# A two-layer diffusion transformer: the first loads cut into quarters of the columns, each with its products, in a written order

## The chip, the cores and the metric

The kernel runs on one core of a Trainium2 chip. The time is device microseconds (us) of that core, lower is better. Five engines work side by side: TensorE (PE: products, transposes), VectorE (DVE), ScalarE (ACT), GpSimd (POOL) and SyncE (SP), each with its own queue that it works off in order; PEld is TensorE's weight load. SP and ACT also start DMA transfers.

## What is computed

Two layers of a hybrid block act on 512 tokens of `x` and 256 context tokens of `ctx`, 1024 columns wide. Each has a SwiGLU feed-forward of half weight, a mixer of four parts (S5 scans, neighbourhood attention, grouped attention, RG-LRU), and another feed-forward. Shifts, scales and gates come from the conditioning vectors. Only the start of the first feed-forward matters here:

```python
def ffn_half(h, g, w_i, w_o, shift, scale, gate):
    y = modulate(rms_norm(h, g), shift, scale)      # rms_norm(h, g) * (1 + scale) + shift
    a, b = jnp.split(y @ w_i, 2, axis=-1)
    return h + FFN_RES * gate * ((jax.nn.silu(a) * b) @ w_o)

ml = ada_mods(silu(c), w_ada[l], b_ada[l], dt)      # mods 0 and 1: shift and scale of 1024 columns each
```

Everything is float32.

## The kernel before

The residual lies in SBUF transposed: eight tiles `e` of 128 columns by 768 tokens (512 latent, 256 context). A float32 product is made of three products of the operands' two parts: high (`wh`, `g` as cast) and low (`wl`, `g` as the difference): hi by lo', lo by hi', hi by hi'. `wload` brings a weight tile, `wsplit` splits it: the cast to `wh` on ACT (L378), the difference `wl` on DVE (L379). There are two buffers each of `wh` and `wl`. `mm` (L389) makes the products.

The feed-forward runs over 22 column tiles `f`. Each has two halves, a and b, in two PSUM tiles `pi` out of two; a half is 8 row blocks x 3 products x 2 pieces. One piece is 258 columns wide (2 for the shifts, of the latent and the context tokens, and tokens 0 to 255), the other 512 (tokens 256 to 767). The RMS factor isn't applied to the input but to the products: `z = pi * R` (L449, L453), where `R` is the factor spread over the partitions. So a `pi` comes free only when `R` is there. `bc` (L448) takes the shifts' products out of `pi`.

At the start the modulations of the first layer are made on TensorE, in two steps of `ada_first`, the scales first and the shifts later. Loads `l`, `z` of 128 x 512 (L206), products with two columns `s` into `pa` (L215), copies to `z` on ACT (L223), transposes to `pt` (L226), sums with the bias to `mods` on DVE (L238). The rows come as 128 tokens x 512 columns (`load_rows`, L168) and are transposed for each of the eight tiles (L178), copied (L180) and squared (`sq_tile`); the squares are summed on DVE. Then `hg_tile` makes the modulated residual's parts: `g` high on ACT (L304), low on DVE (L305). With `in_pair` the first column tile makes its 512-column products of both halves, then calls `setup_rest`, which makes the shifts (`hg_shift`, L291 and L292, the two columns of `g` ahead of the tokens) and the RMS factor (`rms_factor`: `pr` sums over the partitions L357, the inverse root by small steps on DVE L344 to L350, `pb` and its copy to `R` L364 to L366), and then its 258-column products.

The order on each engine is set by a scheduler that moves instructions between the lines as written, by dependencies and its own costs; `tc.keep_in_program_order` (new in the change) keeps an instruction where the program writes it. DMAs on SP and ACT go out in the order of their queue. The S5 coefficients (`S5Coef`, from L1350 on) are made of many small steps on DVE that the scheduler puts where there is room; they are needed much later.

Of the kernel before, what the change touches and what calls it, by code (L numbers as in the profile page):

```python
# [15 lines left out]
P = 128  # L16
D = 1024
NT = D // P
# [16 lines left out]
class Net:  # L35
    def __init__(self, ctx, tc, A, out):
# [11 lines left out]
        self.uid = 0  # L48

# [11 lines left out]
    def setup(self):  # L61
# [22 lines left out]
        scale = self.ada_first(2, 2, "llllllllllllzzzz")  # L84
        raws = [[], []]
        for i, f in enumerate(scale):
            f(0)
            for j in range(6 * i, 6 * i + 6):
                if j < 12:
                    raws[j // 6].append(self.load_rows(j % 6, j // 6))  # L90
        self.load_vectors(0, self.FIRST)
        for f in scale:
            f(1)
        self.transpose_rows(raws)
        gs = self.gain_scale(0, "g_ffn1", 1)
# [18 lines left out]
    def load_rpb(self):  # L114
        """the neighbourhood's biases with something to read before and after them"""
# [13 lines left out]
    def load_vectors(self, l, names=None):  # L129
        """rows to columns; of a layer's rows the first ones or those after them"""  # L130
# [24 lines left out]
        if l == 2:  # L155
            self.s2 = self.const.tile([P, NT, 2], F32, name="s2")
            for i in range(2):
                nc.scalar.activation(self.s2[:, :, i], self.cols[2][:, 8 * i:8 * i + 8], AF.Silu)

# [4 lines left out]
    def load_rows(self, t, b):  # L164
        """128 tokens' half"""
        raw = self.t("g")
        src = self.A["x"][0, t * P:(t + 1) * P, :] if t < 4 else self.A["ctx"][0, (t - 4) * P:(t - 3) * P, :]
        self.nc.sync.dma_start(raw[:, :512], src[:, b * 512:(b + 1) * 512])  # L168
        return raw

    def transpose_rows(self, raws):
        nc = self.nc
        self.h = []
        for j in range(NT):
            ps = self.psb.tile([P, 1024], F32, name=self.nm("px"), tag="psb")
            for t in range(6):
                o = (j % 4) * P
                nc.tensor.transpose(ps[:, t * P:(t + 1) * P], raws[j // 4][t][:, o:o + P], self.ident)  # L178
# [1488 lines left out]
```

## Time and profile before

| | |
|---|---|
| median of 3 runs | 2879.89 us (2878.98 to 2880.39) |
| span of the profiled execution | 2877.7 us |
| TensorE busy | 2819.1 us, 98% of the span |
| VectorE busy | 1742.3 us, 61% |
| ACT busy | 906.5 us, 32% |
| GpSimd busy | 757.7 us, 26% |

The profile is of one execution. Its times are microseconds from the start of the span. TensorE's clock is shown as granted, 1.00 is 2.4 GHz and 0.50 is 1.2 GHz. A plain float32 product on TensorE (`pa`, `pt`, `pr`, `pb`) stands in the trace as two passes, a product of two parts (`pi`) as one.

### The profile page before, as it was taken

The numbers are of one execution on the slowest core, as the hardware profiler recorded it, in microseconds if no ns is written. First come the engines' busy times: TensorE is split into PE (matmuls) and PEld (weight loads), VectorE is DVE, ScalarE is ACT, GpSimd is POOL, SyncE is SP. The second block draws the span as 40 slices with busy tenths as digits, with TensorE's granted clock in tenths as the row PEclk, the third lists the DMA queues.
The fourth block names the chain that finished last, engine by engine and source line by source line (L and its number), as shares of the span: only waits on it lengthen the run. The fifth ranks groups of instructions, "written<-read, shape, count | busy, mean of one in ns | idle before, by whom it ended". The sixth has DMA issues, their size and how long they took to land.

```text
span 2877.7 us, 43478 instructions
## 1 busy us (share of the span) xinstructions
PE 2819.1 (98%) x17293; PEld 2437.7 (85%) x17293; DVE 1742.3 (61%) x3178; ACT 906.5 (32%) x1478; POOL 757.7 (26%) x957
## 2 busy tenths in 40 slices
PE   7999999999999999999999999999999999999998
PEld 4888888888877888888888888888888887899998
DVE  6868577676857566363634766465466876444445
ACT  4212121235546422112123321222224645322223
POOL 2822233221323311000001176332312434201001
PEclk9999999999999999999999999999999999999999
DMA  6445324353323333222311335233254343232231
GB/s 227 134 108 167 112 96 141 123 185 118 115 62 74 103 115 99 87 96 95 107 54 54 118 101 142 80 123 106 74 168 145 118 106 89 79 96 83 88 96 52
DMA packets 295901, 312.13 MB, mean 108 GB/s; under 512 B 58991, under 2 KB 243202, under 8 KB 295698
## 3 DMA queue, kind: packets, MB, share of 16 engines
q1 hardware_dynamic: 266990, 293.97, 31.8%
q0 software_dynamic: 5664, 12.59, 1.9%
q10 hardware_dynamic: 23044, 2.78, 0.7%
q8 instruction: 137, 2.24, 0.3%
q14 instruction: 66, 0.54, 0.1%
HBM read 276.09 MB, written 29.02 MB: 106 GB/s over the span
## 4 chain that ended last, share of the span: by engine, by line
PE 88%; DVE 6%; DMA 2%; ACT 2%; issue 1%; POOL 0%; SPq 0%; ACTq 0%; DVEq 0%; POOLq 0%
PE pi L389 51%; PE po L389 23%; PE po L1236 4%; DVE acc L256 2%; PE po L862 2%; PE pt L810 2%; DMA wa<-in_w_ada_dram 1%; PE ps L793 1%; PE pa L263 1%; DVE wl L379 1%; PE ps L794 1%; DMA l<-in_w_ada_dram 1%; PE pl L734 1%; DVE z L455 0%; PE pa L215 0%
## 5 line engine op out<-in xcount | busy, mean ns | idle before, releaser
L389 PE MATMUL pi<-g,wh 128*128 128x258 f32 (+2 forms) x6656 | 1408.7, 330 | 8.4 <-ACT wh L378 2.6
L389 PEld LDWEIGHTS pi<-g,wh 128*128 128x128 f32 x6656 | 1101.4, 191 | 132.2 <-issue 15.0
L389 PE MATMUL pi<-g,wl 128*128 128x258 f32 (+2 forms) x3328 | 828.1, 329 | 0.7 <-DVE wl L379 0.7
L378 ACT CAST wh<-wr 128x1024 fp32r<-128x1024 f32 (+3 forms) x380 | 338.2, 890 | 1397.4 <-PE pi L389 674.8
L389 PEld LDWEIGHTS pi<-g,wl 128*128 128x128 f32 x3328 | 607.4, 191 | 60.6 <-issue 2.5
L389 PE MATMUL po<-l,wh 128*128 128x512 f32 (+1 forms) x2464 | 566.1, 344 | 0.9 <-DVE e L495 0.8
L389 PEld LDWEIGHTS po<-l,wh 128*128 128x128 f32 x2464 | 387.9, 188 | 63.9 <-issue 3.9
L459 POOL TENSOR_TENSOR l<-z,l 128x768 fp32r<-128x768 f32 (+1 forms) x88 | 159.1, 1808 | 1061.4 <-ACT l L458 955.4
L379 DVE TENSOR_TENSOR wl<-wr,wh 128x1024 fp32r<-128x1024 f32 (+3 forms) x380 | 407.0, 1071 | 50.3 <-ACT wh L378 47.5
L256 DVE SCALAR_TENSOR_TENSOR acc<-wa,s,acc 128x512 f32<-128x512 f32 x448 | 358.6, 849 | 39.4 <-DMA wa<-in_w_ada_dram 38.6
L495 DVE SCALAR_TENSOR_TENSOR e<-po,gt,e 128x512 f32<-128x512 f32 (+1 forms) x296 | 176.2, 631 | 307.4 <-PE po L389 250.7
L389 PE MATMUL po<-l,wl 128*128 128x512 f32 (+1 forms) x1232 | 337.5, 343 | 1.0 <-DVE wl L379 1.0
L453 DVE TENSOR_TENSOR z<-pi,R 128x768 f32<-128x768 f32 (+2 forms) x91 | 78.4, 865 | 301.3 <-PE pi L389 301.3
L389 PEld LDWEIGHTS po<-l,wl 128*128 128x128 f32 x1232 | 194.5, 188 | 32.6 <-DVE wl L379 2.0
L448 DVE COPY bc<-pi 128x2 f32<-128x2 f32 x88 | 13.7, 156 | 189.4 <-PE pi L389 189.4
L458 ACT CAST l<-z 128x768 fp32r<-128x768 f32 (+1 forms) x88 | 68.8, 782 | 160.5 <-DVE z L455 160.5
L1545 POOL TENSOR_TENSOR ww<-AR,BB 128x256 f32<-128x256 f32 x32 | 25.9, 808 | 341.4 <-PE pw L1564 309.5
L455 DVE SCALAR_TENSOR_TENSOR z<-z,pi,z 128x512 f32<-128x512 f32 (+1 forms) x154 | 107.1, 730 | 5.5 <-ACT z L451 0.7
L317 POOL TENSOR_TENSOR ssq<-ssq,sq 128x768 f32<-128x768 f32 (+1 forms) x35 | 67.5, 1929 | 161.0 <-ACT sq L316 161.0
L451 ACT ACTIVATE z<-z,bc 128x512 f32<-128x512 f32 (+1 forms) x154 | 90.0, 625 | 62.7 <-DVE z L449 51.3
L449 DVE TENSOR_TENSOR z<-pi,R 128x768 f32<-128x768 f32 (+1 forms) x88 | 77.5, 880 | 3.7 <-ACT R L366 3.7
L1236 PE MATMUL po<-l,wh 128*128 128x512 f32 (+1 forms) x264 | 71.9, 356 | 0.0
(349 smaller groups left out, 2632.0 us busy)
## 6 DMA issues: line engine op xcount, KB each, us to landing
wr<-in_w_ffn_in_dram SPq DMA_DIRECT2D x88, 1024.0 KB
wa<-in_w_ada_dram SPq DMA_DIRECT2D x64, 1024.0 KB
wr<-in_w_ffn_out_dram SPq DMA_DIRECT2D x48, 512.0 KB
wr<-in_w_ffn_out_dram SPq DMA_DIRECT2D x32, 640.0 KB
wr<-in_w_in_dram SPq DMA_DIRECT2D x16, 1024.0 KB
W<-s5w SPq DMA_DIRECT2D x32, 256.0 KB
wr<-in_w_out_dram SPq DMA_DIRECT2D x8, 1024.0 KB
l<-in_w_ada_dram SPq DMA_DIRECT2D x24, 256.0 KB
```

The source lines that it names most:

```text
L256: nc.vector.scalar_tensor_tensor(acc[r], raw[:, k], s, acc[r], ALU.mult, ALU.add)
L378: nc.scalar.copy(hi[:, :kn], raw[:, :, o:o + P])
L379: nc.vector.tensor_sub(lo[:, :kn], raw[:, :, o:o + P], hi[:, :kn].bitcast(F32))
L389: nc.tensor.matmul(dst, lhsT=wt[:, k, :], rhs=xt[:, a:b], start=(k == 0 and i == 0), stop=(k == kn - 1 and i == 2))
L449: nc.vector.tensor_mul(ta[:, :nt], pa[:, 256:256 + nt], self.R[:, :nt])
L451: nc.scalar.activation(ta[:, a:b], ta[:, a:b], AF.Silu, bias=bc[:, i:i + 1])
L453: nc.vector.tensor_mul(tb[:, a:b], p, self.R[:, a:b])
L455: nc.vector.scalar_tensor_tensor(tb[:, a:b], tb[:, a:b], pb[:, 254 + i:255 + i], ta[:, a:b], ALU.add, ALU.mult)
L458: nc.scalar.copy(uh[:, :nt], tb[:, :nt])
L459: nc.gpsimd.tensor_sub(ul[:, :nt], tb[:, :nt], uh[:, :nt].bitcast(F32))
L495: self.nc.vector.scalar_tensor_tensor(self.h[j][:, a:b], ps[:, a:b], gate[:, j, i:i + 1], self.h[j][:, a:b], ALU.mult, ALU.add)
L1236: self.nc.tensor.matmul(dst, lhsT=wt[:, k, :], rhs=xt[:, a:b], start=(c == 0 and i == 0), stop=(c == NT - 1 and i == 2))
```

## The change

- **Loads.** `ada_first` now makes 256 columns at a time: loads of 3, 3 and 2 row blocks (128x3x256), `pa` of 32 x 256 in strips of 32 rows, one copy to `z` on ACT, and a small product with `sel`, which adds the strips up and transposes in one. The rows come as 256 columns at a time. SP's order is: quarter 0 of the scales, quarter 0 of the rows, the first two weight tiles (128x8x128, of column tile 0 alone), quarters 1 to 3, then the shifts.
- **Scale quarters.** `setup` makes for each quarter the scale, two tiles `e`, two tiles `g`, and the 512-column products of the quarter ahead, in an order pinned on TensorE, ACT and DVE.
- **Shift quarters.** `setup_rest` makes for each quarter the shifts, two times `hg_shift`, and the 12 products of 258 columns. These products are not pinned.
- **Column tiles 0 and 1** have weights of their own, loaded at 128 columns; from tile 2 on the weights come in pairs, as before.
- **Squares** of the first tiles are made where the program has room, and summed on DVE.
- The first steps of the S5 coefficients are pinned, behind the transposes of their rows.

```diff
-        scale = self.ada_first(2, 2, "llllllllllllzzzz")
...
+        scale = [self.ada_first(1024 + 256 * c) for c in range(4)]
+        raws = []
+        for c in range(4):
+            scale[c][0]()
+            raws.append(self.load_rows(c))
+            if c == 0:
+                w_in = self.A["w_ffn1_in"][0]
+                self.first = [self.wload(w_in, 0, NT, o, P) for o in (0, DFF)]
...
+        quarter(0)
+        w = [self.wsplit(raw, NT, 0) for raw in self.first]
+        self.first = [(self.psb.tile([P, 1024], F32, name=self.nm("pi"), tag="psb"), x) for x in w]
+        for c in range(4):
+            for j in (2 * c, 2 * c + 1):
+                self.hg_tile(j, 0, None, gs, TT)
+            if c < 3:
+                quarter(c + 1)
+            for k in (2 * c, 2 * c + 1):
+                for ps, x in self.first:
+                    self.mm(self.in_chunks(ps, TT)[1:], x, self.hgx, NT, k, k + 1, self.pin)
         for j in range(NT):
-            self.hg_tile(j, 0, None, gs, TT)
+            self.sq_tile(j, TT, nc.vector)
 
     def setup_rest(self):
...
-        for f in self.ada_first(0, 4, "l" * 12 + "z" * 4):
-            f()
-        for j in range(NT):
-            self.hg_shift(j, 0, 0)
+
+        nc = self.nc
+        shift = [self.ada_first(256 * c) for c in range(4)]
+        for load, _ in shift:
+            load()
+        for c, (_, work) in enumerate(shift):
+            work()
+            for j in (2 * c, 2 * c + 1):
+                self.hg_shift(j, 0, 0)
+                for ps, x in self.first:
+                    self.mm(self.in_chunks(ps, TT)[:1], x, self.hgx, NT, j, j + 1)
         self.rms_factor(TT)
...
+        def work():
+            ps, arow = self.bank("pa")[:, :256], self.t("z")[:, :256]
+            for k in range(NT):
+                o = 32 * (k % 4)
+                self.pin(nc.tensor.matmul(ps[o:o + 32], lhsT=self.s2w[:, 2 * k:2 * k + 32], rhs=w[k], start=(k < 4), stop=(k >= 4)))
+            self.pin(nc.scalar.copy(arow, ps))
+            pt = self.bank("pt", "pst")[:, :4]
+            for b in range(2):
+                self.pin(nc.tensor.matmul(pt[:, 2 * b:2 * b + 2], lhsT=arow[:, b * P:(b + 1) * P], rhs=self.sel, start=True, stop=True))
+            self.ada_add(0, c0 // P, [pt.rearrange("p (q b r) -> p q b r", q=1, r=2)], self.pin)
```

ACT's order where the residual's parts begin. Before, all eight tiles' copies and squares, and the scales, stand ahead of this place:

```order
L223 COPY z_184<-pa_167 2x512 x2
L304 ACTIVATE g_290<-e_201,gs_288 128x512
L304 ACTIVATE g_290<-e_201,gs_288 128x256
L378 CAST wh_350<-wr_346 128x1024
L304 ACTIVATE g_296<-e_211,gs_288 128x512
L304 ACTIVATE g_296<-e_211,gs_288 128x256
L304 ACTIVATE g_302<-e_223,gs_288 128x512
L304 ACTIVATE g_302<-e_223,gs_288 128x256
L378 CAST wh_354<-wr_348 128x1024
```

After, the same place on ACT, from the first weight on (`ssq` takes the first tile's squares, `sq` the others'; `lrow` and `dt` are small loads for the S5 coefficients):

```order
L400 CAST wh_203<-wr_127 128x1024
L245 COPY z_166<-pa_165 128x256
L1374 DMA lrow_963<-in_s_lambda_im_dram 32x64
L1376 DMA dt_968<-in_s_log_step_dram 128x32
L400 CAST wh_207<-wr_129 128x1024
L213 COPY e_181<-px_182 128x512
L335 ACTIVATE ssq<-e_181 128x768
L213 COPY e_192<-px_193 128x512
L338 ACTIVATE sq_424<-e_192 128x768
L326 ACTIVATE g_213<-e_181,gs_164 128x512
L326 ACTIVATE g_213<-e_181,gs_164 128x256
```

Both casts of weights now stand ahead of the first copy of `e`, and the copy of the first scales stands behind the first cast.

TensorE's order at the shifts. Before, one block of sums for all shifts, then the roots' sums `pr`, then all 258-column products (the order goes on so to the 34th of them, where `pb` stands):

```order
L215 MATMUL pa_416<-z_449,s_102 2x512
L215 MATMUL pa_416<-z_451,s_102 2x512
L226 MATMUL pt_463<-ident,z_457 128x128 x4
L357 MATMUL pr_486<-ones,ssq 128x1 x6
L389 MATMUL pi_358<-g_291,wh_350 128x258
L389 MATMUL pi_358<-g_290,wl_351 128x258
L389 MATMUL pi_358<-g_290,wh_350 128x258
```

After, between the products of quarter 0 and of quarter 1 of the shifts, on TensorE:

```order
L411 MATMUL pi_212<-g_219,wl_208 128x258
L411 MATMUL pi_212<-g_219,wh_207 128x258
L244 MATMUL pa_508<-l_459,s2w 32x256 x3
L244 MATMUL pa_508<-l_461,s2w 32x256 x3
L244 MATMUL pa_508<-l_463,s2w 32x256 x2
L248 MATMUL pt_519<-sel,z_509 128x2 x2
L411 MATMUL pi_211<-g_276,wh_203 128x258
L411 MATMUL pi_211<-g_275,wl_204 128x258
```

Each quarter's sums now stand behind the products of the quarter ahead of it.

VectorE's order from the end of the roots on. Before, the last steps of the inverse root (`rs_t`, `r`), then the first tile's evacuation, and the next weights behind it:

```order
L348 SCALAR_TENSOR_TENSOR rs_t_495<-r_104_493 128x6
L349 TENSOR_TENSOR rs_t_495<-rs_t_495,rs_v_494 128x6
L350 SCALAR_TENSOR_TENSOR r_104_493<-rs_t_495,r_104_493 128x6
L448 COPY bc_612<-pi_358 128x2
L449 TENSOR_TENSOR z_613<-pi_358,R 128x768
L379 TENSOR_TENSOR wl_627<-wr_346,wh_626 128x1024
L453 TENSOR_TENSOR z_614<-pi_359,R 128x768
```

After, VectorE from `bc` on (`wl_698` and `wl_751` are the low parts of column tile 1's two weights):

```order
L465 COPY bc_679<-pi_211 128x2
L372 SCALAR_TENSOR_TENSOR r_117_608<-rs_t_610,r_117_608 128x6
L370 SCALAR_TENSOR_TENSOR rs_t_610<-r_117_608 128x6
L371 TENSOR_TENSOR rs_t_610<-rs_t_610,rs_v_609 128x6
L372 SCALAR_TENSOR_TENSOR r_117_608<-rs_t_610,r_117_608 128x6
L370 SCALAR_TENSOR_TENSOR rs_t_610<-r_117_608 128x6
L401 TENSOR_TENSOR wl_698<-wr_693,wh_697 128x1024
L371 TENSOR_TENSOR rs_t_610<-rs_t_610,rs_v_609 128x6
L401 TENSOR_TENSOR wl_751<-wr_695,wh_750 128x1024
L372 SCALAR_TENSOR_TENSOR r_117_608<-rs_t_610,r_117_608 128x6
L180 COPY cols_88<-pv_651 128x40
```

`bc` and the two `wl` have moved into the chain of the inverse root, ahead of its last step.

## Rows read from the trace of the kernel before

**Rows 1.** The page: the span, and busy time and share of each engine.

```profile
span 2877.7 us, 43478 instructions
...
PE 2819.1 (98%) x17293; PEld 2437.7 (85%) x17293; DVE 1742.3 (61%) x3178; ACT 906.5 (32%) x1478; POOL 757.7 (26%) x957
```

**Rows 2.** Windows: stretch, length, busy us by engine, granted clock, DMA share, GB/s.

```profile
core 0: us, PE busy (x) PEld busy (x) DVE busy (x) ACT busy (x) POOL busy (x), PEclk, DMA share, GB/s
0.00:5.00 5.00, 0.00 (x0) 0.00 (x0) 0.27 (x7) 1.28 (x1) 1.08 (x7) 1.00 0.60 190
5.00:10.00 5.00, 3.38 (x9) 0.53 (x9) 0.18 (x1) 0.31 (x2) 0.00 (x0) 1.00 0.83 253
10.00:15.00 5.00, 4.58 (x23) 2.68 (x21) 1.20 (x2) 2.29 (x4) 0.00 (x0) 1.00 0.86 272
...
30.00:35.00 5.00, 2.27 (x4) 0.88 (x5) 4.51 (x8) 4.84 (x8) 0.00 (x0) 0.72 1.06 405
...
60.00:65.00 5.00, 4.44 (x21) 4.36 (x22) 3.90 (x22) 0.57 (x7) 4.47 (x10) 0.50 0.00 0
80.00:100.00 20.00, 20.00 (x114) 17.29 (x113) 19.68 (x63) 5.11 (x6) 17.22 (x34) 1.00 0.34 107
100.00:150.00 50.00, 49.70 (x286) 42.67 (x284) 39.92 (x78) 10.61 (x15) 46.97 (x103) 1.00 0.42 122
```

**Rows 3.** TensorE's timeline: start, duration, line, tile, count; idle before it in brackets.

```profile
22.45 0.87 PE L178 MATMUL px<-ident,g 128*128 128x128 f32 x6
...
32.26 0.80 PE L389 MATMUL pi<-g,wh 128*128 128x512 f32 x1 [2.56 <-ACT wh L378]
...
58.36 0.66 PE L226 MATMUL pt<-ident,z 128*128 128x128 f32 x4 [2.52 <-ACT z L223]
...
61.37 0.58 PE L389 MATMUL pi<-g,wh 128*128 128x258 f32 x1 [0.56 <-DVE g L292]
...
464.41 0.64 PE L263 MATMUL pa<-acc,ones 128*32 128x256 f32 x8
```

**Rows 4.** Groups by line and shape: busy us, mean ns, idle before.

```profile
L378 ACT CAST wh<-wr 128x1024 fp32r<-128x1024 f32 x224 | 235.3, 1050 | 896.9 <-PE pi L389 518.7 <-issue 187.8 <-PE po L389 115.1
L305 DVE SCALAR_TENSOR_TENSOR g<-e,gs,g 128x512 fp32r<-128x512 f32 x48 | 36.9, 768 | 0.2 <-ACT g L304 0.2
L316 ACT ACTIVATE sq<-e 128x768 f32<-128x768 f32 x35 | 29.0, 832 | 3.4 <-DVE ssq L317 1.8 <-DVE e L180 1.5
L265 ACT COPY z<-pa 128x256 f32<-128x256 f32 x32 | 11.7, 366 | 5.3 <-PE pa L263 5.3
L291 ACT CAST g<-mods 128x2 fp32r<-128x2 f32 x48 | 7.7, 189 | 18.7 <-PE pi L389 13.7 <-PE ps L794 3.5 <-DVE mods L238 1.4
```

**Rows 5.** Timelines of ACT and of VectorE: start, duration, line, tile, count.

```profile
35.09 5.17 ACT L304 ACTIVATE g<-e,gs 128x512 fp32r<-128x512 f32 x10
...
64.86 0.17 DVE L350 SCALAR_TENSOR_TENSOR r<-rs_t,r 128x6 f32<-128x6 f32 x1
```

**Rows 6.** The chain of waits from 40 to 75 us: start, duration, what.

```profile
45.95 7.21 PE pi L389 x30
...
59.02 1.80 PE pr L357 x12
...
61.37 6.56 PE pi L389 x34
67.93 0.91 PE pb L364 x8
...
68.86 0.87 ACT R L366 x2
...
69.75 0.96 DVE z L449
70.71 1.23 DVE wl L379
...
71.98 3.10 PE pi L389 x16
```

More of the change, by code (lines that the diff above doesn't have):

```diff
@@ L48, in __init__ @@
         self.uid = 0
+        self.pin = tc.keep_in_program_order
     def t(self, tag, dt=F32):
@@ new lines, in setup, with quarter @@
+        scale = [self.ada_first(1024 + 256 * c) for c in range(4)]
[6 more added lines that the diff above has]
+                self.first = [self.wload(w_in, 0, NT, o, P) for o in (0, DFF)]
+        self.h = []
+        gs = self.small.tile([P, NT, 2], F32, name="gs0", tag="gs", bufs=2)
+        def quarter(c):
+            scale[c][1]()
+            j = slice(2 * c, 2 * c + 2)
+            g = self.col(0, "g_ffn1", 0, 8)[:, j].unsqueeze(2).to_broadcast([P, 2, 2])
+            self.pin(nc.vector.scalar_tensor_tensor(gs[:, j], self.mods[0][:, 8 + 2 * c:10 + 2 * c, :], 1.0, g, ALU.add, ALU.mult))
+            for i in range(2):
+                self.transpose_rows(raws[c], i)
@@ L232, in ada_add, with load @@
-    def ada_add(self, l, c, parts):
+        w = []
+        def load():
+            src = self.A["w_ada"][0, :, c0:c0 + 256].rearrange("(k p) c -> p k c", p=P)
+            for a, b in ((0, 3), (3, 6), (6, 8)):
+                t = self.t("l")[:, :(b - a) * 256].rearrange("p (k c) -> p k c", c=256)
+                nc.sync.dma_start(t, src[:, a:b])
+                w.extend(t[:, i] for i in range(b - a))
+        def work():
[8 more added lines that the diff above has]
+            self.ada_add(0, c0 // P, [pt.rearrange("p (q b r) -> p q b r", q=1, r=2)], self.pin)
@@ L234, in ada_add @@
+        return load, work
+    def ada_add(self, l, c, parts, then=lambda i: i):
         n = parts[0].shape[1] * parts[0].shape[2]
@@ L237, in ada_add @@
         for i, x in enumerate(parts):
-            self.nc.vector.tensor_tensor(out, x, out if i else bias, ALU.add)
+            then(self.nc.vector.tensor_tensor(out, x, out if i else bias, ALU.add))
     def ada_steps(self, l, q, ring=None):
@@ L380, in wsplit, with mm @@
         return hi, lo
-    def mm(self, chunks, w, xs, kn):
+    def mm(self, chunks, w, xs, kn, k0=0, k1=None, then=lambda i: i):
         nc = self.nc
         hi, lo = w
-        for k in range(kn):
+        for k in range(k0, k1 or kn):
             xh, xl = xs(k)
@@ L388, in mm @@
                 for dst, (a, b) in chunks:
-                    nc.tensor.matmul(dst, lhsT=wt[:, k, :], rhs=xt[:, a:b], start=(k == 0 and i == 0),
-                                     stop=(k == kn - 1 and i == 2))
+                    then(nc.tensor.matmul(dst, lhsT=wt[:, k, :], rhs=xt[:, a:b], start=(k == 0 and i == 0),
+                                          stop=(k == kn - 1 and i == 2)))
     def hgx(self, k):
@@ L428, in ff_in @@
         def ff_in(f):
-            if f % 2 == 0:
-                pair(f)
-            ra, rb = raws[f - f % 2]
-            o = (f % 2) * P
+            if late and f < 2:
+                ra, rb = [self.wload(w_in, 0, NT, o + P, P) for o in (0, DFF)] if f else (None, None)
+                o = 0
+            else:
+                if f % 2 == 0:
+                    pair(f)
+                ra, rb = raws[f - f % 2]
+                o = (f % 2) * P
             if late and f == 0:
-                pa, pb = self.in_pair(self.wsplit(ra, NT, o), self.wsplit(rb, NT, o), nt, late)
+                late()
+                pa, pb = (ps for ps, _ in self.first)
                 parts = ((0, nt, pb[:, 256:256 + nt]),)
```

106 lines of the change are left out of this document (33 added, 73 removed).

## The prediction, made before the changed kernel ran

> **What bounds the kernel now.** I read four views: the page's busy shares, then busy time by windows from the start on, then the timeline of TensorE, and last the chain of waits up to 75 us. TensorE is busy for 98% of the span [rows 1], and from about 72 us on it hardly waits: 20.00 us of 20 at 80 to 100 us, 49.70 of 50 behind that [rows 2]. So whatever the change does to the start counts one to one up to the moment from which TensorE has gapless work, and that is the third column tile (product tile of f = 1), whose stream is gapless from 71.98 us [rows 6] (its first two products came a little ahead of that). I take 71.5 us as the moment to beat. Only the code ahead of it changes. In the start of before the reader is to see three pieces [rows 3, 6]. First product of 512 columns at 32.26 us, after a TensorE that idled (2.56 us for the cast of wh); last one at 53.16 us (45.95 + 7.21, 0.24 us a product). Then the shifts: passes of pa, copies on ACT, transposes at 58.36 us, pr, and the products of 258 columns from 61.37 us. Then the tail, partly under those products: pb at 67.93, R at 68.86, the first tile's z at 69.75, wl at 70.71, products of the third tile at 71.98.
>
> The profiled span is 2877.7 us [rows 1] and the median of the runs 2879.9 us, so 2.2 us lie around the span. I work on the span and add them. A measurement of this kernel can tell about 0.2%, or 5.8 us, from no change.
>
> **Part 1, loads and scale by quarters: a gain of about 10.5 us at the last 512-column product.** DMA moved 190, 253 and 272 GB/s in the first three windows [rows 2]: 2.2 MB by 10 us. The changed queue puts quarter 0 of the scales (1.05 MB) and of the rows (0.79 MB) and the two first weights (0.52 MB each) first, so the first weight is there at about 10.5 us and the second at 12.4 us. ACT stands in a pinned order with the cast of wh_203 ahead of the copy that the scales wait for, and that of wh_207 ahead of the first copy of e: with 1.05 us a cast [rows 4] ACT begins on e at about 13.5 us. From there ACT sets the pace of a quarter: the copy of z 0.37 us [rows 4]; TensorE's sums and four transposes for e, about 1.2 us (six transposes took 0.87 us [rows 3], the rest is the small products and the steps on VectorE between them); two copies of 512 columns at 0.58 (two thirds of the 0.87 us that the 768 columns of R took [rows 6]); two pairs of g at 1.03 (ten instructions took 5.17 us [rows 5]); two squares at 0.83 [rows 4]. That is 0.37 + 1.2 + 1.16 + 2.06 + 1.66 = 6.45, with hand-offs 7.0 us. Quarter 0 has no wait in it and ends near 18.5 us, quarter 3 at 18.5 + 3 x 7.0 = 39.5. Then VectorE's last low parts (0.77 us for 512 columns [rows 4], 1.5 with the 256) and six products at 0.24: 42.5 us instead of 53.16. Bounds: cycle 6.3 gives 40, cycle 8 gives 45.5. VectorE has some 6 us of work in a quarter (two low parts of 768 columns at 1.2 to 1.5, two sums of squares at 0.96 as z took [rows 6], the copies of e's last 256 columns and small steps), which the 7 us of ACT hide; with no cover the upper bound holds. DMA is not late in this: the last rows are byte 8.4 MB, which at the 272 GB/s is there at 33 us, before ACT's quarter 3 wants them.
>
> A page speaks against the smaller loads. Loads of one size, 256 KB, went at 190 to 272 GB/s up to 15 us and at 405 GB/s at 30 to 35 us [rows 2], so the number in flight mattered here at least as much as the size; the Trainium skill, "DMA: Bandwidth & Descriptors", section "Rules for kernel authors", asks for at least 1 MiB a DMA, and the change has 128 to 512 KB. By that rule the loads would stay at their early rate and the sum would be rival 3's; the 405 GB/s at 256 KB do not bear it out.
>
> **Part 2, shifts by quarters: a loss of about 7 us against the old stage.** On TensorE pa of a quarter of the shifts now stands behind the 12 products of the quarter before it, so nothing overlaps. One quarter: pa 0.64 us (eight passes of the same shape at 464.41 us [rows 3]; that is four products, and there are eight, so twice, overlapped to about 1.1), copy of z 0.37 [rows 4], the two small products and their hand-off 0.6, VectorE's mods 0.17 (the small step at 64.86 us [rows 5]), cast 0.19 [rows 4], subtraction about the same, hand-offs between engines of some 0.05 each, then 12 products of 258 columns at 0.12 (half of the 0.24 for 512): 1.45. Together about 4.25 us; between 3.6 (hand-offs under one another) and 5.0. Before, one such product took 0.19 on the mean, with half the clock in most of them (34 in 6.56 us [rows 6]). Three quarters end at 42.5 + 12.75 = 55.25. The fourth has pr between its small products and its 12 products, 1.80 us [rows 6], which hides the mods and casts: 55.25 + 2.2 + 1.8 + 1.45 = 60.7 us for the last 258-column product.
>
> **Part 3, the tail: a loss of about 4 us.** Before, the roots (rsqrt) ran on VectorE under the products of 258 columns, and pb came after 34 of the 48. Now VectorE's queue has, inside the chain of rsqrt, a copy bc that waits for the very last product of the first half, and behind it two low parts of weights, which wait for casts on ACT, which in turn wait until the last product has read the old weight. After the last product at P: bc and five steps at 0.2 (0.17 each [rows 5]) to P + 1.25; wl 1.23 [rows 6] to P + 2.5; one step, then wl again to P + 3.9; the last step to P + 4.1. pb 0.9, R 0.87, z 0.96 [rows 6], with hand-offs: P + 7.0. Queued behind the waiting wl on VectorE is all that R needs, and everything waits for R. Third tile at 60.7 + 7.0 = 67.7, or 3.8 us earlier than 71.5. The weights of that tile are ready by then, so nothing follows z, which before had wl behind it.
>
> **Part 4, what the idle tail costs: about 2.5 us.** TensorE has only pb and pv to do between P and P + 7. In before it had a like stretch, with gaps of 2.52 and 0.56 us around pt and pr [rows 3], and then showed half the clock, 0.50 at 60 to 65 us [rows 2]: 34 products of 258 columns took 6.56 us [rows 6] instead of 34 x 0.12 = 4.1, 2.5 us more. That was inside the 71.5. Now the same comes behind the third tile's start. Bounds 0 (pb and pv keep the clock) and 3.5 us (the idle stretch here is the longer one).
>
> **Part 5, VectorE's load later: about 1.5 us.** Some 100 small steps of the S5 coefficients that stood on VectorE ahead of the first tile's roots now stand behind the tail. At 0.12 us each (0.17 alone [rows 5], less where they overlap) that is an estimate of 12 us. They fall into tiles in which VectorE has 0.3 us free in 80 to 100 us and 10.1 us free in 100 to 150 us [rows 2], 10.4 in all. What doesn't fit, 1.6 us, delays the release of a bank by z, and TensorE with it. Bounds: 0 (the steps find more room behind 150 us) and 5 us (a third of the free time lies where a step can't use it).
>
> Everything else is worth nothing: no square was left on GpSimd at this place (they are summed on VectorE in before), the reordered rows in the two mixers are the same instructions, and I allow 2 us either way for them. Sum: -3.8 + 2.5 + 1.5 = +0.2 us, so 2877.9 + 2.2 = 2880.
>
> **Rivals.**
> 1. *The quarters are quicker than my sum, and the clock holds (faster).* Cycle 6.3 and shift quarter 3.6: 40 + 3 x 3.6 + 1.9 + 1.8 + 1.45 = 56 us for the last product, tail 6, third tile at 62; 9.5 us gained, less 1.5 to 2.5 for the clock: 2872. For it: the sums add hand-offs that the queues may overlap. Against: ACT's instructions alone are 6.45 us.
> 2. *The clock falls already in the shifts (slower).* The place is the four quarters at 43 to 60 us, in which TensorE has work for 2.6 of 4.25 us. In before windows with it busy for 2.27 of 5 us showed 0.72 [rows 2]. At half clock pa and the 12 products cost 1.9 us more a quarter, 7.6 in all: 2888. It decides the sign if two of the four quarters are hit and VectorE's load costs its upper 5 us. Against: the gaps are about 1 us each, and those before the two falls in before were over 2.
> 3. *The loads bind after all (the change doesn't do what it says).* With 262 GB/s throughout, the last quarter of the shifts (byte 15.3 MB) lands at 58 us instead of being there when TensorE wants it at 55.3: 2.7 us more, 2883, still the same within 0.2%. For it: runs of 512 bytes to 1 KB. Against: 405 GB/s at 30 to 35 us [rows 2].
>
> **How the numbers follow.** Forecast 0.4, with its own range of 2875 to 2885; rival 1 0.27; rival 2 0.25; rival 3 0.08, within the same. So faster 0.27, same 0.46, slower 0.27. The range reaches to both rivals' times, with a little beyond for the unknown load of VectorE: 2871 to 2890.
>
> **What would show it.** The last 512-column product at 42.5 us (40 to 45.5), quarters of shifts 4.25 us apart, the last product of 258 columns at 60.7, pb 4 us behind it, the third tile at 67.7 us with a granted clock of half behind it, and VectorE above 19.7 of 20 us to about 130 us. A granted clock under 0.9 at 45 to 60 us speaks for rival 2; a wait for a DMA ahead of pa for rival 3; a third tile before 64 us for rival 1. If all that is as I say and the time still differs by over 3 us, the cause is behind 75 us, in VectorE's load or in the mixers' order.

## The result, and the profile after

The changed kernel is slower: 2894.32 us (2891.07 to 2900.5, 4 runs) against 2879.43 us for the kernel before beside it, a ratio of 1.0055 with a 95% interval of 1.004 to 1.0069. In a second set, beside the experiments, it took 2889.39 us (2883.14 to 2896.65, 6 runs) against 2880.23, ratio 1.0034 (1.0022 to 1.0046). So its medians lose 9 and 15 us; the prediction said 2880 and a range that ended at 2890. Two executions of it are profiled, with spans of 2889.3 and 2894.9 us; the first is the one read here unless the second is named.

The first two lines of the page answer to [rows 1]:

```profile
span 2889.3 us, 43678 instructions
...
PE 2815.8 (97%) x17381; PEld 2446.4 (85%) x17381; DVE 1744.7 (60%) x3192; ACT 907.4 (31%) x1484; POOL 760.5 (26%) x957
```

TensorE's, VectorE's, ACT's and GpSimd's busy times are those of before within 4 us, over a span that is 11.6 us longer: what has grown is idle time. To see where, take the first product of each phase on TensorE's timeline and subtract. "In" are the products into `pi`, "out" those of the output matrix; a group is a run of column tiles between two residual updates. The columns are microseconds later than in before, for the two profiles of the changed kernel and the runs that are told below.

| phase starts | before | changed | changed, 2nd | e1 | e2 | e4 | e10 | e12 | e7 | e8 | e9 |
|---|---|---|---|---|---|---|---|---|---|---|---|
| out, group 1 | 159.29 | +1.65 | +7.62 | +7.59 | +8.52 | +7.74 | +2.60 | +3.67 | +0.48 | -4.07 | -1.83 |
| in, group 2 | 202.71 | +0.52 | +6.48 | +8.01 | +7.38 | +6.61 | +4.89 | +2.54 | +1.24 | -5.20 | -2.96 |
| out, group 2 | 297.44 | +10.64 | +17.15 | +7.74 | +10.53 | +13.55 | +10.29 | +9.24 | +0.97 | -4.52 | -1.68 |
| out, group 3 | 413.15 | +11.35 | +17.99 | +7.96 | +10.81 | +14.43 | +10.51 | +10.16 | +1.14 | -4.14 | -1.59 |
| out, group 4 | 530.18 | +8.37 | +15.08 | +5.21 | +7.97 | +12.69 | +8.01 | +10.11 | +0.73 | -4.39 | -1.84 |
| layer 2, in, group 2 | 1745.06 | +7.68 | +14.04 | +6.26 | +7.62 | +14.95 | +9.17 | +10.59 | -0.09 | -5.02 | +0.81 |
| layer 2, out, group 2 | 1835.63 | +12.87 | +18.68 | +6.15 | +9.44 | +19.66 | +9.99 | +15.72 | +0.09 | -4.68 | +1.13 |

Read the two columns of the changed kernel downward. Up to 203 us the first profile is where before is, +0.52; the second has lost 6.48. Then both lose the same, 10.12 and 10.67 us, within group 2 (203 to 297 us), and again 5.19 and 4.64 us within group 2 of the second layer. Between 413 and 530 us 3 us come back, since of two waits of before for sums of later modulations (1.48 and 2.09 us) the first is as long (1.49) and the second is 0.46. The start, on which the whole prediction was spent, is not where the steady part of the loss lies.

TensorE's timeline of the changed kernel. The rows are start, duration, line, tile, count, and the idle time ahead:

```profile
14.74 1.01 PE L248 MATMUL pt<-sel,z 128*128 128x2 f32 x4 [3.21 <-ACT z L245]
22.43 0.61 PE L248 MATMUL pt<-sel,z 128*128 128x2 f32 x4 [2.34 <-ACT z L245]
...
45.32 0.39 PE L411 MATMUL pi<-g,wh 128*128 128x512 f32 x1
...
48.51 0.39 PE L411 MATMUL pi<-g,wh 128*128 128x258 f32 x1 [0.67 <-DVE g L313]
...
53.00 0.39 PE L411 MATMUL pi<-g,wh 128*128 128x258 f32 x1 [0.67 <-DVE g L313]
...
63.89 0.28 PE L411 MATMUL pi<-g,wh 128*128 128x258 f32 x1
67.58 2.90 PE L386 MATMUL pb<-ident,r 128*128 128x128 f32 x12 [3.42 <-DVE r L372]
...
72.10 0.62 PE L411 MATMUL pi<-g,wh 128*128 128x258 f32 x2 [0.77 <-DVE z L466]
...
242.33 1.01 PE L411 MATMUL pi<-g,wh 128*128 128x258 f32 x2 [3.33 <-ACT wh L400]
...
295.44 0.62 PE L284 MATMUL pa<-acc,ones 128*32 128x256 f32 x4 [2.15 <-DVE acc L277]
```

The last 512-column product ends at 45.7 us (53.16 in before [rows 6]), the last of 258 columns at 64.2, the third tile begins at 72.10 (71.5). Behind that TensorE waits for only about 1 us in all until 242.33 us, where it waits 3.33 us for the cast of a weight and comes back at half clock (two products in 1.01 us instead of 0.62). At 295.44 it waits again, 2.15 us, for sums of later modulations. In before neither wait is there.

What ACT did before the first of the two waits, from its timeline; rows of "ACTq" are DMA issues in ACT's queue:

```profile
223.21 0.83 ACT L475 CAST l<-z 128x768 fp32r<-128x768 f32 x1 [1.73 <-DVE z L472]
223.81 0.69 ACTq L1451 DMA_DIRECT2D B<-in_s_b_re_dram  x1
...
225.35 7.85 ACTq L1451 DMA_DIRECT2D B<-in_s_b_im_dram  x2
233.24 1.09 ACTq L1454 DMA_DIRECT2D dc<-in_s_d_dram  x1
...
236.42 0.39 ACTq L1461 DMA_DIRECT2D crow<-in_s_c_re_dram  x1
238.88 0.34 ACTq L1462 DMA_DIRECT2D crow<-in_s_c_re_dram  x1
...
240.22 0.72 ACT L468 ACTIVATE z<-z,bc 128x512 f32<-128x512 f32 x1 [15.91 <-DVE BB L1477]
...
241.25 1.03 ACT L400 CAST wh<-wr 128x1024 fp32r<-128x1024 f32 x1
```

ACT computes nothing for 15.91 us, though the Silu's operand had been there since 234.8 us. Its queue holds 13 issues of small loads for the S5 coefficients (`load(0)`: b, d and c of the first direction). Most take 0.3 to 1.1 us, but the two of b's imaginary part take 2.81 and 5.00 us, the 7.85 of the row. Why these two take so long isn't shown: the first carries no wait for a semaphore, and the semaphore of the second had last been raised at 200.8 us. One wait for a DMA is shown: the issue for c at 238.88 stands behind the landing of b at 238.85, after a gap of 2.07 us. In the second profile ACT is held for 15.88 us, 8.61 of it in the same two issues. The Silu and the cast `wh` that TensorE wants stand behind. The row's releaser (BB on VectorE) is only the last semaphore seen; the issues fill the time. Half clock follows, as the windows of the same stretch show (columns as in [rows 2]):

```profile
200.00:225.00 25.00, 25.00 (x144) 20.91 (x143) 20.47 (x29) 5.39 (x7) 21.38 (x51) 1.00 0.48 149
225.00:250.00 25.00, 21.35 (x107) 17.34 (x106) 20.41 (x30) 3.10 (x4) 13.52 (x10) 0.86 0.80 193
250.00:275.00 25.00, 25.00 (x144) 20.92 (x142) 17.20 (x25) 5.18 (x7) 4.70 (x2) 1.00 0.44 149
275.00:300.00 25.00, 22.61 (x125) 18.67 (x124) 22.81 (x31) 4.98 (x8) 15.49 (x16) 0.93 0.35 101
```

Idle time is 3.65 us in the second row and 2.39 in the fourth. The clock of 0.86 and 0.93 is half clock for 28% and 14% of 25 us, half of which is lost: 3.5 and 1.75 us. Together 11.3, for a measured 10.1; the sum is on the high side, since some of the half clock lies in idle time.

The second layer has the same picture with two waits, the first for ACT's cast, the second for the low part made from it:

```profile
1799.25 0.62 PE L411 MATMUL pi<-g,wh 128*128 128x258 f32 x2 [1.90 <-ACT wh L400]
1801.81 1.01 PE L411 MATMUL pi<-g,wl 128*128 128x258 f32 x2 [1.95 <-DVE wl L401]
```

In the kernel before, the same 13 issues stood at 159 to 169 us, in the output products of group 1. This is its ACT, from the same view:

```profile
161.71 2.04 ACTq L1434 DMA_DIRECT2D B<-in_s_b_im_dram  x1
163.80 1.17 ACTq L1437 DMA_DIRECT2D dc<-in_s_d_dram  x1
...
168.40 0.44 ACTq L1445 DMA_DIRECT2D crow<-in_s_c_im_dram  x1
168.94 0.73 ACT L378 CAST wh<-wr 128x640 fp32r<-128x640 f32 x1 [6.41 <-DMA crow<-in_s_c_re_dram]
```

The longest hold of ACT was 6.41 us there, and TensorE was idle for 1 us in that stretch. Why did the issues move? The change pins the first steps of the S5 coefficients (`n.pin` in `base`), and the steps behind them moved on VectorE from ahead of 60 us to 107 us and later; everything that follows from them, the loads included, came a phase later. The order of the built program shows it on ACT, but not at the start. Before:

```order
L265 COPY z_1718<-pa_1717 128x256
L1434 DMA B_251_1728<-in_s_b_re_dram 64x16x16
L1434 DMA B_252_1729<-in_s_b_re_dram 64x16x16
L1434 DMA B_251_1728<-in_s_b_im_dram 64x16x16
L458 CAST l_1701<-z_1693 128x768
```

After, ACT's order has them six casts of output weights (`128x640`) and a column tile further on:

```order
L475 CAST l_2243<-z_2235 128x768
L286 COPY z_2270<-pa_2269 128x256
L1451 DMA B_266_1799<-in_s_b_re_dram 64x16x16
L1451 DMA B_267_1800<-in_s_b_re_dram 64x16x16
L1451 DMA B_266_1799<-in_s_b_im_dram 64x16x16
```

### The profile page after: what moved, and what is told of

Same layout as the page of the kernel before. It is cut to its first block, busy times and chain, and to the rows that moved or that the text cites. A ratio compares the mean times of both kernels' runs of the same rounds, so it can differ in the third digit from the quotient of the medians.

```text
span 2889.3 us, 43678 instructions
## 1 busy us (share of the span) xinstructions
PE 2815.8 (97%) x17381; PEld 2446.4 (85%) x17381; DVE 1744.7 (60%) x3192; ACT 907.4 (31%) x1484; POOL 760.5 (26%) x957
## 5 line engine op out<-in xcount | busy, mean ns | idle before, releaser
L411 PEld LDWEIGHTS pi<-g,wh 128*128 128x128 f32 x6656 | 1104.0, 192 | 133.3 <-issue 11.3
L277 DVE SCALAR_TENSOR_TENSOR acc<-wa,s2w,acc 128x512 f32<-128x512 f32 x448 | 360.6, 851 | 40.7 <-DMA wa<-in_w_ada_dram 40.1
```

What stands on the lines that cost most here:

```text
L277: nc.vector.scalar_tensor_tensor(acc[r], raw[:, k], s, acc[r], ALU.mult, ALU.add)
L411: then(nc.tensor.matmul(dst, lhsT=wt[:, k, :], rhs=xt[:, a:b], start=(k == 0 and i == 0), stop=(k == kn - 1 and i == 2)))
```

## The experiments

Theory A: the steady loss comes from ACT's queue, held by issues of S5's loads at a place where TensorE soon needs ACT. Rival B: the quarters themselves, by gaps or late loads. Rival C: VectorE's moved steps. Theory D, on what differs between the two profiles: the clock in the serial quarters. Times are medians; the ratio is against the kernel before, run beside.

**e1: the first S5 steps not pinned.** 2888.67 us, ratio 1.0027 (1.0017 to 1.0036).

```diff
-            n.pin(nc.tensor.transpose(...))
-        n.exp_small(self.W, dt, dt, n.pin)
-        n.pin(V.tensor_copy(lr, ps[:, 0:32]))
-        n.pin(V.tensor_copy(li, ps[:, 32:64]))
+            nc.tensor.transpose(...)
+        n.exp_small(self.W, dt, dt)
+        V.tensor_copy(lr, ps[:, 0:32])
+        V.tensor_copy(li, ps[:, 32:64])
```

> The changed kernel, but the first steps of the S5 coefficients are no longer pinned; the order then has the 13 small loads of S5's first direction on ACT's queue in the first group's output products again (as before), no longer in the second group's input products. Theory A (in the changed kernel ACT's queue is held at 224 to 240 us by the issues of these loads, the Silu and the cast of the next weight stand behind them, and TensorE waits 3.3 us and drops to half clock): the 10 us between 203 and 308 us are gone, the second group's output products start near 298 us instead of 308, and the time is 2880 to 2886. Rival B (the loss comes from the quarters themselves, whose gaps or late weight loads are paid later): the loss at 203 to 308 us stays, 2892 to 2896. Rival C (VectorE's moved steps are the cause): about half comes back, as the steps are early again, but the tail at 64 to 72 us grows by 2 to 4 us.

The loads are back in the output products (183 to 193 us), and the losses of group 2 are gone in both layers: -0.27 us where the changed kernel loses 10.1, -0.11 where it loses 5.2. That is what theory A asked for, and rival B did not. The start paid for it: VectorE now has the S5 steps inside the tail, `pb` waits for them at 69.38 us, and a stall of 3.04 us at 104.39 behind a full VectorE follows, so that +8.01 us stand at 203 us:

```profile
69.38 2.90 PE L386 MATMUL pb<-ident,r 128*128 128x128 f32 x12 [4.37 <-DVE pwc L1503]
...
104.39 0.98 PE L411 MATMUL pi<-g,wh 128*128 128x258 f32 x2 [3.04 <-DVE z L472]
```

The time is above the 2880 to 2886 of the expectation for that reason. Rival C's 2 to 4 us more in the tail did not come: it takes 8.94 us instead of 7.93, and the third tile begins at 73.95. The rest of what the start lost lies in the stall at 104.39 us and in half clock from 63 to 77 us. ACT is held for 9.23 us at the loads' place, at no cost to TensorE. The time alone (1.0027) doesn't separate e1 from the changed kernel (1.0034 and 1.0055); the table of phases does, and so do the times of e4 and e10 below, which differ in this pin alone.

**e2: S5's small loads on GpSimd's queue.** 2887.33 us, 1.0023 (1.0014 to 1.0032).

```diff
     def load(self, d):
...
-                nc.scalar.dma_start(...)
+                nc.gpsimd.dma_start(...)
```

> The changed kernel with S5's small loads issued from GpSimd's queue instead of ACT's, in both layers; everything else keeps its place. Theory A: ACT no longer stands still at 224 to 240 us nor in the second layer at 1781 to 1797 us; 8 to 10 us come back in the first, up to 5 in the second: 2879 to 2884. Rival B: the weight itself is late or the stream is behind for another reason, so nothing changes: 2892 to 2896. A lesser outcome (2885 to 2890) would say that VectorE's steps that wait for these loads hold the products too.

The loads are the same and go through another queue (GpSimd starts transfers too), but two more things differ. They go out later, at 237.8 to 248.1 us, behind work of GpSimd's own, and from 235 us on the order on VectorE and TensorE is another one. Group 2 loses 3.15 us instead of 10.1 to 10.7, the second layer 1.82 instead of 4.6 to 5.2. What stays in group 2 are three waits of about 1 us for later modulations' sums at 272 to 296 us, and in the second layer one of 2.15 us for VectorE at 1798.51. So most of the loss went through ACT's queue. The rest is the expectation's lesser outcome (2885 to 2890), in which VectorE's steps hold the products too. The time didn't fall to 2879 to 2884, since in the profiled execution over 5 us were lost at the start (third tile at 77.48 us): the granted clock fell to half within the shift quarters (columns as in [rows 2]):

```profile
50.00:55.00 5.00, 3.83 (x40) 2.57 (x35) 0.42 (x3) 0.66 (x3) 0.00 (x0) 0.87 0.09 26
55.00:60.00 5.00, 3.81 (x24) 2.84 (x17) 0.42 (x3) 0.66 (x3) 0.00 (x0) 0.50 0.00 0
60.00:65.00 5.00, 4.51 (x30) 2.94 (x28) 0.22 (x2) 0.65 (x3) 0.00 (x0) 0.50 0.00 0
65.00:70.00 5.00, 4.84 (x22) 4.54 (x22) 1.71 (x12) 0.78 (x2) 0.00 (x0) 0.50 0.00 0
```

Up to 235 us this program's order of instructions is that of the changed kernel on every engine, and the changed kernel's two profiles show 1.00 at 50 to 65 us.

**e3 and e6: the loads' late place alone, in the kernel before.** e3 holds back the four loads of b: 2880.51 us, 1.0000 (0.9991 to 1.0009). e6 holds back b and c, 12 of the 13: 2879.63 us, 0.9999 (0.999 to 1.0007).

```diff
+        if l == 0 and d == 0:
+            for x in self.B:                       # and of the tiles for c
+                nc.scalar.copy(x[:, 0:1], n.mark)  # n.mark: a column of column tile 6's product
...
-S5_FIRST = (1, 1, 4)
+S5_FIRST = (1, 1, 5)
```

> The kernel before, with one thing of the change done alone: the four loads of S5's b of the first direction stand on ACT's queue where the changed kernel has them, in the second group's input products (the loads of c stay early). Theory A: ACT stands still near 224 us, TensorE waits for the weight's cast, and the kernel is 4 to 10 us slower: 2884 to 2890. Rival B: without the quarters nothing is lost, 2878 to 2882.

> The kernel before with the small loads of S5's first direction, b and c (12 of 13), held back to where the changed kernel has them on ACT's queue, in the second group's input products; ten copies of one column on ACT hold them there. With the four loads of b alone nothing was lost, since ACT was held for 6 us and had 6 to 7 us of slack. Theory A: with all of them ACT is held for 10 us or more, a Silu and a cast of a weight come late, TensorE waits 2 to 4 us and restarts at half clock: 4 to 9 us slower than before, 2885 to 2890, all of it between 203 and 308 us. Rival (the place of these loads costs only together with the quarters' start): within 2 us of before.

Both miss theory A's number. The diff is that of e6; `S5_FIRST` says behind which column tiles the program writes the first S5 steps. ACT's timeline in e6 says why:

```profile
222.80 3.76 ACTq L1439 DMA_DIRECT2D B<-in_s_b_im_dram  x2
...
231.00 0.39 ACTq L1456 DMA_DIRECT2D crow<-in_s_c_im_dram  x1
231.43 1.05 ACT L378 CAST wh<-wr 128x1024 fp32r<-128x1024 f32 x1 [4.27 <-DMA crow<-in_s_c_im_dram]
...
232.88 1.12 ACT L451 ACTIVATE z<-z,bc 128x512 f32<-128x512 f32 x2 [0.40 <-DVE acc L256]
```

The issues hold ACT from 220.9 to 231.4 us, 10.5 us, and the Silu was not due before 232.9. In the changed kernel they hold it from 223.8 to 240.2, since the two issues of b take 7.85 us instead of 3.76 and one of c waits over 2 us; the Silu had been due at 234.8. In e6 ACT also computes between its issues: the cast of the next weight comes ahead of the Silu, and the longest idle times are 3.89 and 4.27 us instead of 15.91. So the late place by itself costs nothing here. What makes b's two issues take twice as long in the changed kernel isn't shown. Theory A stands, corrected: not the place, but the hold beyond the slack.

**e4: the RMS factor ahead of the shifts.** 2895.2 us, 1.0052 (1.0037 to 1.0066).

```diff
+        self.rms_factor(TT)
         for c, (_, work) in enumerate(shift):
...
-        self.rms_factor(TT)
```

> The changed kernel with the RMS factor made ahead of the shift quarters instead of behind them (sums, roots, pb and R on record before the first shift). It tests the tail by itself: in the changed kernel the last product of 258 columns ended near 64 us and the third tile began at 72.1. Prediction's part 3 (the tail costs 7 us since R waits for the low parts of weights): the third tile begins 5 to 6 us earlier, near 66.5 us, and the second group's output products come 5 to 6 us earlier, at 302 to 303 us: 2886 to 2890. Rival: the time went elsewhere, as the front is hidden by a later wait: the third tile is earlier, but the second group's products are not, 2892 to 2896.

`pb` stands at 46.98 us now, hidden, and the third tile began at 70.13 us though the clock was at half from 62 us on; e2, at half clock too and with the old tail, began it at 77.48. So the tail's 7 us were real: here TensorE idles 0.56 us ahead of the third tile. Group 2 still lost 6.94 us and the second layer 4.71. The rival was right on the total: VectorE then waited 8.67 us for a 1 MB load, with the copies that free a `pi` behind it, and TensorE stalled 4.09 us at 155.57:

```profile
150.28 0.75 DVE L277 SCALAR_TENSOR_TENSOR acc<-wa,s2w,acc 128x512 f32<-128x512 f32 x1 [8.67 <-DMA wa<-in_w_ada_dram]
```

This wait is in every profile, and in several it decides over the start's gain. In before it is 5.85 us and costs 0.38; in the changed kernel 5.31 and 0.52 (in the second profile 7.19 and 2.41); in e8 7.01 and 2.60, in e7 7.66 and 2.96. Where TensorE stalls behind it, the stall is the wait less 3.7 to 5.5 us; in e1, e2, e10 and e6 waits of 5.1 to 6.0 us cost nothing. From issue to landing that load took 5.8 us in before and 7.8 and 9.7 in the two profiles of the changed kernel, where 0.78 MB of S5's tables, eight of 95 KB, go by GpSimd's queue beside it; in before there are none in that stretch. Over all 14 profiles it took 5.1 to 6.2 us with none of the tables beside it (before, e1, e3, e6, e11), 5.7 to 7.6 with four (e7, e9, e10) and 7.0 to 9.7 with eight (the changed kernel, e2, e4, e8, e12, all with S5 pinned). So the pinned steps bring the tables to this load too. That is a comparison of kernels that differ in more; no run moves the tables alone.

**e5: the changed kernel again.** 2889.39 us, as told above.

> The changed kernel itself once more, beside the others on one chip. Theory D (the granted clock in the shift quarters is not settled by the code: at 3.8 us of work in 5 it holds in some executions and falls in others): its times spread over some 8 to 10 us (2887 to 2898) where the kernel before spreads over 7, and if the profiled execution shows half clock anywhere from 50 to 80 us, its third tile starts 4 to 6 us after 72.1 and the later stages are shifted by as much. If the clock always holds, the profile repeats 72.1 us within 0.5 and the spread is that of the kernel before.

The spread is 13.5 us (6 runs) where before has 7.4 (29 runs), as theory D says. But in this profile it wasn't the shift quarters whose clock fell (1.00 up to 70 us); it fell behind the tail, 0.55 at 70 to 75 us, and the third tile began at 73.34, 1.2 us later where theory D expected 4 to 6. A lower clock within the shifts was seen in e1 (0.79 to 0.87), e2 (0.50), e4 (0.66 and 0.50) and e10 (0.67 and 0.50), all with serial quarters, and in none of the four runs with the sums together. Theory D holds for the kind of kernel, and is not shown for the changed kernel's own two executions.

**e10 and e12: parts of the start.** e10 has S5's steps free and the RMS factor first: 2887.05 us, 1.0022 (1.0014 to 1.0031). Against e4 (1.0037 to 1.0066) only the pin is gone, and the intervals don't meet. e12 has one edit on the changed kernel, the sums of all four shift quarters ahead of the first 258-column product: 2893.73 us, 1.0041 (1.0029 to 1.0054). Both are slower than expected (2878 to 2880 and 2883 to 2890).

```diff
-        for c, (_, work) in enumerate(shift):
-            work()
+        for _, work in shift:
+            work()
+        for c in range(4):
             for j in (2 * c, 2 * c + 1):
```

> The run e7 without one of its three edits: the sums pa of the shift quarters stand again behind the products of the quarter ahead (S5's steps free, RMS factor first). What the four serial quarters cost by themselves: by the prediction's part 2 a quarter takes 4.25 us, four of them 17, against about 11 when the sums stand together: 5 to 6 us over e7, 2878 to 2880. If the sums together gain nothing, since the copies and casts are the longer chain: within 2 us of e7.

> The changed kernel with one edit: the sums pa of all four shift quarters ahead of the first 258-column products. Front: third tile 5 to 6 us earlier than in the changed kernel at the same clock. The small loads of S5 stay where they are, so theory A expects the loss of 7 to 11 us between 203 and 308 us and of 5 us in the second layer to be there still: 2883 to 2890. If that loss was due to the state of the start (half clock and late loads there) and not to ACT's queue, it shrinks with it: 2876 to 2882.

e12's third tile began at 66.05 us, 6 earlier than in the changed kernel, and was at +2.54 us at 203 us: a stall of 5.35 us at 151.88 behind a wait of VectorE of 9.04 us took most of it. Then it lost 6.7 us in group 2 and 5.1 in the second layer, as theory A said, but not where theory A had it. ACT was held for 13.10 us, and TensorE behind it lost only 0.39 and 0.85 us, at full clock. Most of the loss is the second wait, with half clock behind it:

```profile
243.46 0.62 PE L412 MATMUL pi<-g,wl 128*128 128x258 f32 x2 [0.85 <-DVE wl L402]
...
292.50 1.07 PE L285 MATMUL pa<-acc,ones 128*32 128x256 f32 x4 [2.15 <-DVE acc L278]
```

e4 is alike (0.35 and 0.85 us, then 2.16 at 296.83). So the second wait doesn't hang on the first stall. With the loads off ACT's queue it is 1.03 us in e2 and 0.67 in e8, and the clock holds; no run separates how the queue lengthens it. e10 gave a third place for theory A. Its S5 issues stand at the end of the output products, hold ACT for 11.89 us, and TensorE waits at the seam to group 2:

```profile
206.50 2.00 ACT L400 CAST wh<-wr 128x1024 fp32r<-128x1024 f32 x2 [11.89 <-DMA crow<-in_s_c_re_dram]
```

```profile
207.60 1.01 PE L411 MATMUL pi<-g,wh 128*128 128x258 f32 x2 [3.26 <-ACT wh L400]
...
210.71 0.98 PE L411 MATMUL pi<-g,wh 128*128 128x258 f32 x2 [2.10 <-DVE e L512]
```

It loses 2.3 us at the seam and 5.4 in group 2, with half clock for 9.57 us.

**e7, e8, e9: RMS factor first, sums together, and S5 in three ways.** e7 (S5 free, RMS factor first, sums together): 2873.39 us, 0.9981 (0.9972 to 0.999). e8 (as e7, but S5 pinned and its loads on GpSimd's queue): 2877.19 us, 0.9987 (0.9979 to 0.9996). e9 (e7 with the loads on GpSimd's queue): 2874.81 us, 0.9982 (0.9973 to 0.9991).

> The changed kernel with S5's first steps not pinned, the RMS factor made ahead of the shifts, and the sums pa of all four shift quarters ahead of the first 258-column products. If the causes add up (S5's loads back in the output products: -10 in group 2 and up to -5 in the second layer; tail hidden: -5; four serial quarters replaced by one: -6), the third tile starts near 62 to 65 us and the time is 2872 to 2879. If VectorE or a wait for a load in its queue takes the time back (as the changed order did at other places): third tile early, but a stall of 3 us or more between 80 and 160 us, 2880 to 2888.

> As the run before it, but with S5's first steps pinned as in the changed kernel and S5's small loads on GpSimd's queue instead. If ACT's queue is the whole of the loss at 203 to 308 us, and the front gains as in the run before: 2872 to 2880. If what is left at 250 to 300 us with the loads on GpSimd (three waits of 1 us for the sums of later modulations) stays: 2878 to 2884.

> The run e7 (S5's first steps not pinned, RMS factor ahead of the shifts, sums of all shifts first; 2873.4 us) with S5's small loads on GpSimd's queue too. If ACT's queue still costs something there (second layer, or the output products of the first group): 2868 to 2872. If the place of the loads was the whole of it, they cost nothing where e7 has them: 2872 to 2875.

e7 and e9 beat the kernel before by 0.18 to 0.19%, e8 by 0.13%. Against e10, e7 is 0.41% or 12 us faster, but not all of that is the sums together. In the profiles e7 is 3.65 us ahead of e10 at 203 us, 2.3 of which is e10's loss at the seam, and the other 5.7 us come in group 2, where e7 loses nothing (-0.27). The windows of e7 (columns as in [rows 2]):

```profile
50.00:55.00 5.00, 4.81 (x54) 3.62 (x55) 0.83 (x6) 1.20 (x7) 0.00 (x0) 1.00 0.16 48
55.00:60.00 5.00, 5.00 (x51) 4.35 (x50) 2.12 (x18) 0.91 (x4) 0.00 (x0) 1.00 0.00 0
60.00:65.00 5.00, 2.75 (x16) 1.98 (x16) 4.89 (x32) 3.64 (x8) 0.00 (x0) 0.99 0.03 7
65.00:70.00 5.00, 4.10 (x13) 3.54 (x14) 5.00 (x25) 1.02 (x2) 0.68 (x1) 0.50 0.60 193
```

TensorE is full at 50 to 60 us and keeps its clock, where e10 was busy for 3.34 of 5 us and dropped to 0.67 and 0.50. The third tile begins at 63.44 us, 8 earlier than in before, and yet at 203 us e7 stands at +1.24 in its profile: half clock at 65 to 70 us, the stall at 149, and 1.61 us at 198.94 for a `wl` behind a hold of ACT of 8.17 us. e9 differs from e7 by less than the interval of 0.09% (2.6 us), so ACT's queue costs at most that where e7 has the loads. e8 has S5 pinned, as the changed kernel, but not its loads in ACT's queue, and loses 0.68 us in group 2 and 0.34 in the second layer.

**e11: the kernel before with S5's loads on GpSimd's queue.** 2882.53 us, 1.0006 (0.9997 to 1.0015): the same.

> The kernel before with S5's small loads on GpSimd's queue, nothing else. If ACT's queue is held in before only where nothing waits (its output products in the first layer, 9.7 us of ACT without TensorE waiting in the second): same as before within 3 us, 2877 to 2883. If it costs there too: faster by 3 us or more.

So ACT's queue was no loss in before within 0.15%, though it was held there too.

## Why the prediction was wrong

**The step that failed is the line "Everything else is worth nothing".** It counted the steps of the S5 coefficients as work that VectorE gets back later, and not as the head of a chain whose 13 DMA issues stand in ACT's queue. In their new place, with longer issues, they hold ACT for 15.91 us, and group 2 loses 10.1 and 10.7 us, the second layer 5.2 and 4.6. Without the pin (e1) this is -0.27 and -0.11; with the pin and the loads on GpSimd's queue (e2) 3.15 and 1.82. Without these losses the first profile would have ended a few us below before. The sign that the prediction gave for this, a cause behind 75 us, held, but not the place it named, VectorE's load or the mixers' order. I read the order only at the start and called the rest the same; ACT's rows behind the first group would have told.

**Part 1, first loads: mechanism right, term 3 us too good.** 45.7 us instead of 42.5, just outside the bounds of 40 to 45.5. The first cast of a weight began at 13.37 us (10.5 expected), since its load, issued at 7.78 us, landed only at 13.35; the second landed at 15.09 (12.4). By then 3.2 MB had moved, and the prediction had the weight complete at 2.4 MB: loads that were issued behind it moved beside it. So "DMA is not late in this" failed for the first weights. The first copy of `e` came at 16.74 (13.5). From there the copies of `z` for quarters 1 to 3 came at 22.03, 30.04 and 36.32 us: cycles of 8.0 and 6.3, a mean of 7.15 for 7.0. The slow one has the transposes at half clock.

**Part 2, shift quarters: right.** 48.51 to 53.00 to 57.51 us is 4.5 a quarter (4.25). The last product ended at 64.2 us, 3.5 later than forecast, of which 3.2 are part 1.

**Part 3, tail: right in its mechanism, 0.9 us too short.** 7.9 us instead of 7.0. VectorE's two `wl` ended at 67.3 us, `pb` began 3.4 us behind the last product (4.1 forecast), but took 2.1 us up to R's first copy (0.9 forecast), at a clock that was falling. VectorE's rows:

```profile
66.14 1.22 DVE L401 TENSOR_TENSOR wl<-wr,wh 128x1024 fp32r<-128x1024 f32 x1
67.28 0.16 DVE L372 SCALAR_TENSOR_TENSOR r<-rs_t,r 128x6 f32<-128x6 f32 x1
...
71.09 0.95 DVE L466 TENSOR_TENSOR z<-pi,R 128x768 f32<-128x768 f32 x1
```

**Part 4, the idle tail's clock: within its bounds, and different in the two executions.** In the first profile half clock lay in `pb` (0.76 at 65 to 70 us) and the third tile ran at full clock; in the second it lay at 70.5 to 77.3 us (0.55 at 70 to 75, 0.76 at 75 to 80), of which 4.0 us are behind the third tile's start at 73.34: 2.0 us lost there. The forecast had 2.5 in bounds of 0 to 3.5.

**Part 5, VectorE's load: no stall in the first profile.** VectorE was busy for 42.29 of 50 us at 100 to 150 us, TensorE for 50.00. The steps fitted. What I had not seen is that VectorE's queue also holds a wait for a 1 MB load, 5.85 us in before, just within its slack; in the second profile and in e4, e7, e8 and e12 it was longer, and stalls of 2.4 to 5.4 us came off the start's gain.

**The sum at 203 us** was forecast at +0.2 us and was +0.5 in one profile and +6.5 in the other. The +0.5 is luck: the third tile began 4.4 us later than forecast, and the 4.0 us that parts 4 and 5 add behind it did not come there.

**Rivals.** Rival 1 fell: the third tile began at 72.10. Rival 2 (half clock in the shifts) had the sign right and the place wrong for the profiled executions; e2 and e10 show that it happens. Rival 3 was not seen ahead of any `pa` of the shifts: the idle times there are 0.5 us for the copy of `z`. The loads in pieces of 128 to 512 KB moved 317 GB/s at 10 to 15 us, more than the 272 of before, but 268, 348, 350 and 364 in the four windows from 15 to 35 us, where before has 383, 395, 386 and 405 [rows 2]. The Trainium skill, "DMA: Bandwidth & Descriptors", section "Rules for kernel authors", asks for at least 1 MiB a DMA; no run here changes the size alone, so none shows what that rule is worth.

**What stays open.** Why the granted clock falls in the serial quarters in some executions and not in others; why b's two issues hold ACT for 7.85 us in one place and 3.76 in another; how ACT's queue lengthens the second wait in group 2; whether the tables alone make the load `wa` land 2 to 4 us later; and how much of the median's loss beyond the first profile's 11.6 us each of the two carries.

## What to carry to other kernels

When a change pins or delays one early step, follow everything that hangs on it to the end of its chain, in the order of every engine, and mark the DMA issues that stand in the queue of an engine that computes: ask what is behind them and when it is due. A wait that costs nothing in a profile may sit just inside its slack, so note for each long hidden wait how many microseconds it has left. A gain at the start is worth what is left of it at the next such wait; compare phase starts down the whole timeline before you say where time went.

## What the runs showed of the hardware

- DMA issues in ACT's queue held ACT for 16 us in the changed kernel: 13 issues, most of 0.3 to 1.1 us and two of 2.81 and 5.00. With the same loads in GpSimd's queue, where they also went out 14 us later, the loss in that phase fell from 10.1 to 3.15 us.
- A 1 MB load took 5.1 to 6.2 us from issue to landing where none of S5's small tables moved beside it (5 profiles), 5.7 to 7.6 with four of 95 KB (3), 7.0 to 9.7 with eight (6), at the same place in the program.
- With TensorE busy for 3.3 to 3.8 us in 5, the granted clock stayed at 1.00 in two executions of the changed kernel and fell to 0.50 in e2's, in programs of the same order up to there. Kernels with the shifts in serial quarters spread over 9 to 14 us between runs (4 to 12 runs each), those with the sums together over 8 to 10 (5 to 11), the kernel before over 7 to 10 (27 to 29 runs).
